# A decoder trunk on one core: three steps of the other half's background work per pair of up products instead of two, and pooling products issued one group later

## The chip, the cores and the metric

The kernel is one launch on 1 core of a Trainium2 chip. The metric is the device time of that core in microseconds (us): the median of three runs is 2252.49 us (2251.87 to 2254.62).

## What is computed

Two layers over 1040 tokens (16 learned meta tokens and 1024 inputs) with 1024 channels, all in f32. Layer 0 mixes with multi-head latent attention, layer 1 with a causal pooling mixer; each is followed by a gated MLP with a causal convolution of width 3 on the up projection. Cut to what matters here:

```python
for i in range(DEPTH):                               # DEPTH = 2
    a = rmsnorm(h, norm_mix_pre[i])
    m = mla_mixer(a, ...) if i % 2 == 0 else pool_mixer(a, w_group, scale)
    h = h + rmsnorm(m, norm_mix_post[i])
    f = conv_ffn(rmsnorm(h, norm_ffn_pre[i]), ffn_w_up[i], conv_w, conv_b, ffn_w_down[i])
    h = h + rmsnorm(f, norm_ffn_post[i])

def pool_mixer(h, w_group, scale):                   # 4 groups of 256 channels, windows 2, 4, 8, 16
    pooled[:, :, g] = mean of the last POOL_WINDOWS[g] tokens (fewer at the start)
    y = einsum('blgc,gcd->blgd', pooled - h, w_group)
    return y * scale

def conv_ffn(h, w_up, conv_w, conv_b, w_down):       # D_FF = 2816
    u = conv_b + causal width-3 convolution of (h @ w_up)
    gate, val = split(u)
    return (silu(gate) * val) @ w_down
```

## The kernel before

Channels lie on the 128 partitions, tokens on the free axis. Every f32 operand of a product is split into a high and a low part (ACT casts the high part, DVE subtracts to get the low part), and a product of two tiles is three matmuls: high by high, low weight with high data, high weight with low data. So each weight tile that arrives (`wtile`, line 702) costs one cast on ACT (`wh`) and one subtraction on DVE (`wl`), four buffers each.

From line 599 on the program treats the tokens as two halves, half 0 with 536 and half 1 with 504. For each layer and half, `ffn_up` makes the 22 channel tiles of the gated product in two parts of 11 pairs (one gate and one value tile); a pair is two up products on PE and, on DVE, two `wl`, four convolution steps `cv`, one multiplication and one `gl`. `ffn_down` follows each part. While PE works on one half, the other half's non-matrix work (normalisations, residual additions, the pooling mixer) is a generator in the list `bg`; each call of `tick` (line 639) advances it to its next `yield`, at a raised priority, and `drain` runs what is left. `ffn_up` ticks twice in a pair of products. The generator of a half at the layer boundary is `after_ffn`: `post` (line 817, 8 steps), one norm (4 steps), `poolmix` (line 973, 12 steps), then `post` and one norm again.

A norm is `inv_rms_a` (line 75: eight tiny matmuls into `ps_st`, then some ten short DVE operations) and `inv_rms_b` (line 103: two diagonal tiles `diag`, one on DVE and one on POOL, which two or four matmuls into `ps_bc` spread over the partitions; ACT copies the result to `R`). `poolmix` makes, for each of the eight channel tiles, a scaled tile `pa`, one to four running sums `psm`, the difference `pmx` and its parts `xh` and `xl`; after two tiles come the products of that group (`pool` below: matmuls whose operands are `xh`, `xl`, `pwh`, `pwl`), and ACT reads them out into `F`.

The order on each engine is fixed when the program is built: a scheduler places the instructions by priority, and on the chip each engine takes its instructions in that order. Two more sizes matter: the sums of half 1 have six banks of PSUM, those of half 0 three double ones; and the pooling weights have one buffer.

Two places at the layer boundary come up below. Stage A is `ffn_up` of half 1, part 0, layer 0, with half 0's layer boundary behind it (about 1040 to 1200 us). Stage B is `ffn_up` of half 0, part 0, layer 1, with half 1's (about 1440 to 1630 us). A third, stage 0, is `ffn_up` of half 0, part 0, layer 0 (about 620 to 760 us), which has half 1's `after_mixer` behind it.

Of the kernel before, what the change touches and what calls it, by code (L numbers as in the profile page):

```python
# [11 lines left out]
F32 = mybir.dt.float32  # L12
F32R = mybir.dt.float32r
I32 = mybir.dt.int32
ALU = mybir.AluOpType
# [6 lines left out]
KD = D // 128  # L22
# [7 lines left out]
HALF = 536  # L30
# [9 lines left out]
G_MIXPRE, G_MIXPOST, G_FFNPRE, G_FFNPOST = 0, 16, 32, 48  # L40
G_QN, G_KVN, G_PS = 64, 67, 69
G_CONV = 77
G_CNT = G_CONV + 2 * 2 * NJ * 4
# [3 lines left out]
class Kern:  # L47
# [551 lines left out]
    def dense(self):  # L599
        tc, nc, io, ctx = self.tc, self.nc, self.io, self.ctx  # L600
        P = lambda name, bufs, **kw: ctx.enter_context(tc.tile_pool(name=name, bufs=bufs, reuse_waits="tile", **kw))
        self.wp, self.ab, self.hp, self.gp = P("wp", 4), P("ab", 1), P("hp", 1), P("gp", 1)
        self.fp, self.up, self.tp = P("fp", 8), P("up", 2), P("tp", 5)
        stp = P("stf", 2, space=PSUM)
        self.stps = lambda name: stp.tile([128, 512], F32, tag="st", name=name)
        self.psum = None
        self.banks(1)
        self.dtile = lambda x: self.tp.tile([128, HALF], F32R, tag="x" + x, name="diag", bufs=2)
        self.H, self.A, self.bg = {}, {}, []

        F, acc = self.wo(0)
        self.bg.append(self.after_mixer(0, F, acc, 0, True))
        F, acc = self.wo(1)
        self.drain()
        self.bg.append(self.after_mixer(1, F, acc, 0, False))
        for L in range(2):
            self.L = L
            for hf in range(2):
                self.banks(2 - hf)
                Fa = None  # L620
                for part in range(2):
                    G = self.ffn_up(hf, part)
                    self.drain()
                    if part == 1 and hf == 0:
                        self.bg.append(self.pre(1, L))
                    if part == 1 and hf == 1 and L == 0:
                        self.bg.append(self.pre(0, 1))
                    if (L, hf, part) == (1, 1, 1):
                        self.ffn_down_last(part, G, Fa)
                        break  # L630
                    F, acc = self.ffn_down(part, G, Fa)
                    Fa = F
                    self.drain()
                else:
                    self.bg.append(self.after_ffn(hf, F, acc, L))
        self.drain()
# [13 lines left out]
    def after_mixer(self, hf, F, acc, L, pre):  # L650
        acc = yield from self.post(hf, F, acc, G_MIXPOST + 8 * L)
        if pre:

            self.late = yield from self.inv_rms_steps(acc, "xh", 2)
            yield from self.pre(hf, L, True)
        else:
            yield from self.ffn_norm(hf, acc)
# [220 lines left out]
    def ffn_up(self, hf, part):  # L878
        nc, io, L = self.nc, self.io, self.L
        ah, al = self.A[hf]  # L880
        gh, gl = [], []

        cut = hf == 0 and L == 1
        skip = DEAD - 2 if cut else 0
        pad = 2 if cut or hf else 0
        n = ah[0].shape[1] - skip - pad
        for jj in range(JH):
            j = part * JH + jj
            cv = []
            for gv in range(2):  # L890
                idx = gv * NJ + j
                u, = self.mm_half(self.wtile(io["w_up"][L, j, :, gv], KD), ah, al, skip=skip)
                if (L, hf) == (0, 0):
                    t = self.up.tile([128, HALF], F32, tag="u", name="u")
                    nc.vector.tensor_tensor(t, u, self.late, op=ALU.mult)
                    u = t
                p0 = G_CONV + (L * 2 * NJ + idx) * 4
                c = self.tp.tile([128, HALF], F32, tag="t", name="cv")[:, :n]
                nc.scalar.activation(c, u[:, pad:pad + n], AF.Identity, bias=self.par(p0 + 3), scale=self.par(p0 + 2))  # L899
                for x in (1, 0):  # L900

                    o = max(0, 2 - x - pad)
                    nc.vector.scalar_tensor_tensor(c[:, o:], u[:, pad + x - 2 + o:pad + x - 2 + n], self.par(p0 + x),  # L903
                                                   c[:, o:], op0=ALU.mult, op1=ALU.add)
                cv.append(c)
                if gv == 0:
                    nc.scalar.activation(c, c, AF.Silu)  # L907
                    self.tick()
            nc.vector.tensor_tensor(cv[0], cv[0], cv[1], op=ALU.mult)  # L909
            hi = self.gp.tile([128, HALF], F32R, tag=f"gh{jj}", name="gh")[:, :n]  # L910
            lo = self.gp.tile([128, HALF], F32R, tag=f"gl{jj}", name="gl")[:, :n]
            self.split(cv[0], hi, lo, lo_eng="dve")
            gh.append(hi)
            gl.append(lo)
            self.tick()
        return gh, gl
# [56 lines left out]
    def poolmix(self, hf, R):  # L973
        nc, io = self.nc, self.io
        F, acc = [], None
        n_tok = HALVES[hf][1]
        end = n_tok + 16
        for g in range(4):
            win = 2 << g
            xh, xl = [], []  # L980
            for kk in range(2):
                k = 2 * g + kk
                a = self.tp.tile([128, HALF + 16], F32, tag="tc", name="pa")[:, :end]
                if hf == 0:
                    nc.gpsimd.memset(a[:, :16], 0.0)
                else:
                    nc.gpsimd.tensor_scalar(a[:, :16], self.phalo[:, k], 1.0, 0.0, op0=ALU.mult, op1=ALU.add)
                nc.vector.scalar_tensor_tensor(a[:, 16:], self.H[hf][k], self.par(G_MIXPRE + 8 + k), R,
                                               op0=ALU.mult, op1=ALU.mult)
                if hf == 0:  # L990
                    nc.gpsimd.tensor_scalar(self.phalo[:, k], a[:, n_tok:end], 1.0, 0.0,
                                            op0=ALU.mult, op1=ALU.add)
                s = a
                for l in range(g + 1):
                    d = 1 << l
                    lo, hi = 2 * d - 1, end
                    n = self.tp.tile([128, HALF + 16], F32, tag="tc", name="psm")[:, :end]
                    nc.vector.tensor_tensor(n[:, lo:hi], s[:, lo:hi], s[:, lo - d:hi - d], op=ALU.add)
                    s = n
                mx = self.tp.tile([128, HALF + 16], F32, tag="tc", name="pmx")[:, :end]  # L1000
                nc.vector.scalar_tensor_tensor(mx[:, 16:], s[:, 16:], 1.0 / win, a[:, 16:],
                                               op0=ALU.mult, op1=ALU.subtract)
                if hf == 0:
                    nc.vector.tensor_tensor(mx[:, 16:32], s[:, 16:32], self.par(G_CNT + 16 * g, 16), op=ALU.mult)
                    nc.vector.tensor_tensor(mx[:, 16:32], mx[:, 16:32], a[:, 16:32], op=ALU.subtract)
                hi_ = self.tp.tile([128, HALF], F32R, tag="xh", name="xh", bufs=2)[:, :n_tok]
                lo_ = self.tp.tile([128, HALF], F32R, tag="xl", name="xl", bufs=2)[:, :n_tok]
                self.split(mx[:, 16:], hi_, lo_, lo_eng="dve")
                xh.append(hi_)
                xl.append(lo_)  # L1010
                if kk == 0:
                    W = self.wtile(io["w_pool"][g], 4, True)
                yield
            for m in range(2):
                ps = self.mm_half([W[2 * kk + m] for kk in range(2)], xh, xl)
                f = self.fp.tile([128, HALF], F32, tag="F", name="F")[:, :n_tok]
                self.evac(f, ps, self.par(G_PS + 2 * g + m))
                F.append(f)
                acc = self.addsq(acc, f)
            yield  # L1020
        return F, acc


# [50 lines left out]
```

## Time and profile before

| | |
|---|---|
| median of three runs | 2252.49 us (2251.87 to 2254.62) |
| the profiled execution | 2249.77 us, of which 2247.6 us are its span |
| PE busy | 2154.6 us, 96% of the span |
| DVE busy | 1473.8 us, 66% |
| ACT busy | 1048.6 us, 47% |
| POOL busy | 415.5 us, 18% |
| mean granted TensorE clock | 0.983 of full |

The span is the time from the first to the last instruction on the core; 2.2 us of the run's own time lie outside it. A busy engine is not the same as a needed one: the averages go over stages with different limits.

### The profile page before, as it was taken

What the parts mean: (1) busy time and instruction counts of PE and PEld (TensorE: products, weight loads), DVE (VectorE), ACT (ScalarE), POOL (GpSimd) and SP (SyncE); (2) the same over time, 40 slices, a digit from 0 to 9 for tenths busy, and PEclk for the clock granted to TensorE, in tenths of its full rate; (3) what the DMA queues carried; (4) which work ended last, traced back from release to release, by engine and by line L of the source; (5) the groups of instructions that cost most, each with busy time, mean ns of one, the idle gap of its engine ahead of it and who ended that gap; (6) DMA issues with size and microseconds to landing.
All of it is one profiled execution on the core that took longest, in us unless ns stands there. A gap on an engine that the chain in (4) does not pass through costs nothing.

```text
span 2247.6 us, 36505 instructions
## 1 busy us (share of the span) xinstructions
PE 2154.6 (96%) x13968; PEld 1968.5 (88%) x13968; DVE 1473.8 (66%) x2830; ACT 1048.6 (47%) x1934; POOL 415.5 (18%) x755
## 2 busy tenths in 40 slices
PE   8889999998999999999998999999899999999996
PEld 8778888897989999999886888899899998888886
DVE  7867777776388725765887555587745557634655
ACT  6466777776354423443544344344433433433431
POOL 6667676764000000000000000000000000000001
PEclk9989999998999999999999999999999999999998
DMA  5011111114343232233222332422242245223321
GB/s 162 15 44 26 33 30 33 30 55 125 122 159 124 77 99 98 85 95 117 91 80 92 131 101 84 132 79 86 81 135 90 72 132 178 86 84 112 98 91 46
DMA packets 82903, 202.76 MB, mean 90 GB/s; under 512 B 10548, under 2 KB 31668, under 8 KB 82728
## 3 DMA queue, kind: packets, MB, share of 16 engines
q1 hardware_dynamic: 82584, 200.18, 28.5%
q8 instruction: 110, 1.80, 0.3%
q14 instruction: 65, 0.53, 0.1%
q10 hardware_dynamic: 144, 0.25, 0.0%
HBM read 179.15 MB, written 16.97 MB: 87 GB/s over the span
## 4 chain that ended last, share of the span: by engine, by line
PE 85%; DVE 6%; ACT 3%; POOL 2%; issue 2%; DMA 2%; DVEq 0%; SPq 0%; ACTq 0%; POOLq 0%
PE ps_m L756 72%; PE ps_t L577 2%; PE ps_s L525 1%; PE ps_o L562 1%; PE ps_o L563 1%; PE ps_s L527 1%; PE ps_s L526 1%; ACT P L540 1%; PE ps_qk L408 1%; POOL P L545 1%; PE ps_qk L410 1%; DMA xt<-in_x 1%; PE ps_qk L409 1%; PE ps_st L82 1%; DVE ps_s L534 1%
## 5 line engine op out<-in xcount | busy, mean ns | idle before, releaser
L70 DVE TENSOR_TENSOR wl<-wr,wh 128x1024 fp32r<-128x1024 f32 (+3 forms) x316 | 349.3, 1105 | 419.6 <-ACT wh L64 408.6
L64 ACT CAST wh<-wr 128x1024 fp32r<-128x1024 f32 (+3 forms) x316 | 301.2, 953 | 590.8 <-PE ps_m L756 524.1
L756 PE MATMUL ps_m<-ah,wh 128*128 128x506 f32 (+2 forms) x2112 | 563.9, 321 | 3.4 <-ACT cv L899 1.7
L756 PE MATMUL ps_m<-al,wh 128*128 128x506 f32 (+2 forms) x2112 | 566.7, 322 | 0.0
L756 PE MATMUL ps_m<-ah,wl 128*128 128x506 f32 (+2 forms) x2112 | 563.1, 321 | 0.0
L756 PEld LDWEIGHTS ps_m<-ah,wh 128*128 128x128 f32 x2112 | 353.1, 189 | 35.0 <-ACT cv L899 1.9
L756 PEld LDWEIGHTS ps_m<-al,wh 128*128 128x128 f32 x2112 | 352.8, 189 | 28.2 <-issue 0.7
L756 PEld LDWEIGHTS ps_m<-ah,wl 128*128 128x128 f32 x2112 | 353.1, 189 | 27.8 <-issue 0.5
L756 PE MATMUL ps_m<-gh,wh 128*128 128x268 f32 (+3 forms) x1088 | 288.7, 318 | 1.9 <-ACT F L765 1.9
L756 PE MATMUL ps_m<-gh,wl 128*128 128x268 f32 (+3 forms) x1088 | 287.8, 317 | 0.0
L756 PE MATMUL ps_m<-gl,wh 128*128 128x268 f32 (+3 forms) x1088 | 287.3, 317 | 0.0
L903 DVE SCALAR_TENSOR_TENSOR cv<-ps_m,params,cv 128x504 f32<-128x504 f32 (+1 forms) x264 | 195.9, 744 | 3.2
L756 PEld LDWEIGHTS ps_m<-gh,wh 128*128 128x128 f32 x1088 | 182.9, 189 | 16.0 <-ACT F L765 2.1
L756 PEld LDWEIGHTS ps_m<-gh,wl 128*128 128x128 f32 x1088 | 181.9, 188 | 14.2 <-issue 0.5
L756 PEld LDWEIGHTS ps_m<-gl,wh 128*128 128x128 f32 x1088 | 182.1, 189 | 13.1
L115 POOL TENSOR_TENSOR diag<-ident,yl 65x260 fp32r<-65x260 f32 (+5 forms) x27 | 33.5, 1241 | 714.5 <-DVE yl L70 675.3
L64 ACT CAST gh<-cv 128x504 fp32r<-128x504 f32 (+2 forms) x88 | 54.6, 622 | 168.8 <-DVE cv L909 168.8
L540 ACT ACTIVATE P<-ps_s,stat 116x116 f32<-116x116 f32 (+9 forms) x160 | 111.3, 697 | 38.4 <-DVE stat L538 28.1
L577 PE MATMUL ps_t<-ident,P 116*116 116x116 f32 x720 | 118.5, 269 | 7.8 <-DVE ptl L591 4.2
L545 POOL TENSOR_SCALAR P<-P,stat 116x116 f32<-116x116 f32 (+2 forms) x144 | 108.8, 757 | 59.0 <-DVE stat L543 47.3
L907 ACT ACTIVATE cv<-cv 128x504 f32<-128x504 f32 (+2 forms) x88 | 55.8, 634 | 135.2 <-DVE cv L903 135.2
L534 DVE CUSTOM_DVE_ANT_0 ps_s<-ps_s,mask 116x116 f32<-116x116 f32 (+7 forms) x128 | 89.9, 704 | 22.6 <-PE ps_s L527 12.1
(200 smaller groups left out, 3624.3 us busy)
## 6 DMA issues: line engine op xcount, KB each, us to landing
wr<-in_w_up SPq DMA_DIRECT2D x176, 512.0 KB, 3.5
wr<-in_w_down SPq DMA_DIRECT2D x56, 384.0 KB, 3.1
wr<-in_w_down SPq DMA_DIRECT2D x56, 320.0 KB, 2.9
wr<-in_w_o SPq DMA_DIRECT2D x16, 512.0 KB, 4.0
resid<-H SPq DMA_DIRECT2D x16, 268.0 KB, 4.3
H<-resid SPq DMA_DIRECT2D x16, 268.0 KB, 3.1
xt<-in_x SPq DMA_DIRECT2D x32, 130.0 KB, 2.2
resid<-H SPq DMA_DIRECT2D x16, 252.0 KB, 3.6
```

Of the source, the lines that this page charges most:

```text
L64: nc.scalar.copy(hi, src)
L70: eng.tensor_tensor(lo, src, hi.bitcast(F32), op=ALU.subtract)
L82: nc.tensor.matmul(ps[:w, i:i + 1], acc[:, w * i:w * i + w], self.ones, start=True, stop=True)
L115: eng.tensor_tensor(t, self.ident[:w, :w].unsqueeze(1).broadcast_to([w, n, w]), part.bitcast(F32).unsqueeze(2).broadcast_to([w, n, w]), op ...
L408: nc.tensor.matmul(ps, wh, xh, start=i == 0, stop=False)
L534: nc.vector.tensor_tensor_reduce(out=ps, in0=ps, in1=self.mask[:n, o:o + nb * cn].rearrange("p (b c) -> p b c", b=nb), op0=ALU.add, op1=AL ...
L540: nc.scalar.activation(dst, ps, AF.Exp, bias=nm[:n], scale=SCALE, accum_out=es[:n, gi:gi + 1])
L545: nc.gpsimd.tensor_scalar(P[:n, :nk], P[:n, :nk], rs[:n], 1.0, op0=ALU.mult, op1=ALU.mult)
L577: nc.tensor.transpose(pt[:kn, x * QT:x * QT + n], Pi[:n, k0:k0 + kn], self.ident[:n, :n])
L756: nc.tensor.matmul(p, w, x[k][:, skip + c0:skip + c0 + m], start=k == 0 and w is wh and x is xh, stop=k == last and w is wl)
L903: nc.vector.scalar_tensor_tensor(c[:, o:], u[:, pad + x - 2 + o:pad + x - 2 + n], self.par(p0 + x), c[:, o:], op0=ALU.mult, op1=ALU.add)
L907: nc.scalar.activation(c, c, AF.Silu)
```

## The change

`ffn_up` makes each up product in two calls of four weight tiles each, and in the value product of a pair one more `tick` stands between the two, so a pair has three. The matmuls of a product and their order within it are the same. In `poolmix` the body for one channel tile becomes `shape`, and the loop runs one round more: the products of a group stand behind the first tile of the next group, which leaves nine `yield`s instead of twelve. The temporary `u` moves from a pool of its own to the tag `xl`, and `xh` and `xl` have three buffers instead of two. Lines of the changed file lie some lines lower (the convolution is line 907 instead of 903, `pa` 992 instead of 988, `psm` 1002 instead of 998).

```diff
@@ dense
-        self.fp, self.up, self.tp = P("fp", 8), P("up", 2), P("tp", 5)
+        self.fp, self.tp = P("fp", 8), P("tp", 5)
...
-        self.dtile = lambda x: self.tp.tile([128, HALF], F32R, tag="x" + x, name="diag", bufs=2)
+        self.dtile = lambda x: self.tp.tile([128, HALF], F32R, tag="x" + x, name="diag", bufs=3)
@@ ffn_up
-                u, = self.mm_half(self.wtile(io["w_up"][L, j, :, gv], KD), ah, al, skip=skip)
+                W = self.wtile(io["w_up"][L, j, :, gv], KD)
+                ps = self.mm_half(W[:KD // 2], ah, al, 0, KD, skip=skip, n=n + pad)
+                if gv == 1:
+                    self.tick()
+                u, = self.mm_half(W[KD // 2:], ah, al, KD // 2, KD, ps, skip, n + pad)
                 if (L, hf) == (0, 0):
-                    t = self.up.tile([128, HALF], F32, tag="u", name="u")
+                    t = self.tp.tile([128, HALF], F32, tag="xl", name="u", bufs=3)
@@ poolmix (shape(g, kk) holds the old body for one channel tile, unchanged but for bufs=3)
+        X = [([], []) for _ in range(4)]
+        W = None
+        for g in range(5):
             for kk in range(2):
+                if g < 4:
+                    for dst, t in zip(X[g], shape(g, kk)):
+                        dst.append(t)
+                    yield
+                if g and kk == 0:
+                    for m in range(2):
+                        ps = self.mm_half([W[2 * x + m] for x in range(2)], *X[g - 1])
+                        f = self.fp.tile([128, HALF], F32, tag="F", name="F")[:, :n_tok]
+                        self.evac(f, ps, self.par(G_PS + 2 * (g - 1) + m))
+                        F.append(f)
+                        acc = self.addsq(acc, f)
+                if g < 4 and kk == 0:
                     W = self.wtile(io["w_pool"][g], 4, True)
-                yield
...
+        yield
         return F, acc
```

What this does to the order on the engines is shown at three places, in rows that name line, operation, result, operands and size; `x2` means that two equal ones follow each other.

First, PE in stage 0, at the norm whose scale is `R` for half 1's up operand. Before, its sums stand inside an up product:

```order
L756 MATMUL ps_m_10378<-al_9384,wh_10373 128x268 x2
L82 MATMUL ps_st_10200<-ones_66,acc_9841 63x1 x8
L756 MATMUL ps_m_10378<-ah_9383,wl_10374 128x268 x2
L756 MATMUL ps_m_10378<-ah_9389,wh_10373 128x268 x2
L756 MATMUL ps_m_10378<-al_9390,wh_10373 128x268 x2
```

and the norm's first `ps_bc` matmul follows 146 up matmuls later. In the changed program, at the end of a product, stands:

```order
L756 MATMUL ps_m_10247<-al_9447,wh_10242 128x268 x2
L756 MATMUL ps_m_10247<-ah_9446,wl_10243 128x268 x2
L82 MATMUL ps_st_10003<-ones_66,acc_9741 63x1 x8
L122 MATMUL ps_bc_10109<-diag_10105,ones_r_68 128x504
L122 MATMUL ps_bc_10109<-diag_10107,ones_r_68 128x504
L756 MATMUL ps_m_10309<-ah_9368,wh_10304 128x268 x2
```

The 146 up matmuls between the two halves of the norm are gone from there; they stand behind it.

Second, PE in stage A, at the norm before `poolmix`. Before, the spreading matmuls are followed by the rest of their up product and by two more products, 54 matmuls, ahead of the first pooling matmul, and 53 up matmuls stand between the sums and the spreading:

```order
L756 MATMUL ps_m_14420<-al_13362,wh_14415 128x506
L122 MATMUL ps_bc_14406<-diag_14402,ones_r_68 128x268
L122 MATMUL ps_bc_14410<-diag_14402,ones_r_68 128x268
L756 MATMUL ps_m_14420<-ah_13361,wl_14416 128x506
L122 MATMUL ps_bc_14406<-diag_14404,ones_r_68 128x268
L122 MATMUL ps_bc_14410<-diag_14404,ones_r_68 128x268
L756 MATMUL ps_m_14420<-ah_13453,wh_14415 128x506
```

In the changed program 14 up matmuls stand between the sums and the spreading, and the first pooling matmuls follow at once:

```order
L756 MATMUL ps_m_14391<-ah_13459,wl_14387 128x506
L122 MATMUL ps_bc_14251<-diag_14247,ones_r_68 128x268
L122 MATMUL ps_bc_14255<-diag_14247,ones_r_68 128x268
L122 MATMUL ps_bc_14251<-diag_14249,ones_r_68 128x268
L122 MATMUL ps_bc_14255<-diag_14249,ones_r_68 128x268
L756 MATMUL ps_m_14421<-xh_14305,pwh_14329 128x268
L756 MATMUL ps_m_14422<-xh_14305,pwh_14329 128x268
L756 MATMUL ps_m_14440<-xh_14305,pwh_14329 128x268
L756 MATMUL ps_m_14441<-xh_14305,pwh_14329 128x268
L756 MATMUL ps_m_14488<-ah_13190,wh_14483 128x506
```

From there to the last pooling matmul of the half PE had 240 other matmuls (222 of up products and 18 of the down product) among the 96 of pooling; now it has 98.

Third, DVE in stage A, in the third pooling group. Before, the tiles of `poolmix` alternate with the convolution and the weight splits of the up products:

```order
L988 SCALAR_TENSOR_TENSOR pa_14893<-H_13853,params_70,R_14401 128x536
L903 SCALAR_TENSOR_TENSOR cv_14884<-ps_m_14859,params_70,cv_14884 128x504
L1004 TENSOR_TENSOR pmx_14839<-psm_14837,params_70 128x16
L998 TENSOR_TENSOR psm_14897<-pa_14893 128x551
L909 TENSOR_TENSOR cv_14824<-cv_14824,cv_14884 128x504
L1005 TENSOR_TENSOR pmx_14839<-pmx_14839,pa_14829 128x16
L70 TENSOR_TENSOR wl_15300<-wr_15298,wh_15299 128x640
L998 TENSOR_TENSOR psm_14899<-psm_14897 128x549
```

In the changed program they follow each other there:

```order
L1002 TENSOR_TENSOR psm_14594<-psm_14592 128x545
L1005 SCALAR_TENSOR_TENSOR pmx_14596<-psm_14594,pa_14586 128x536
L992 SCALAR_TENSOR_TENSOR pa_14640<-H_13852,params_70,R_14246 128x536
L1008 TENSOR_TENSOR pmx_14596<-psm_14594,params_70 128x16
L1002 TENSOR_TENSOR psm_14644<-pa_14640 128x551
L1009 TENSOR_TENSOR pmx_14596<-pmx_14596,pa_14586 128x16
L1002 TENSOR_TENSOR psm_14646<-psm_14644 128x549
L70 TENSOR_TENSOR xl_14601<-pmx_14596,xh_14600 128x536
L1002 TENSOR_TENSOR psm_14648<-psm_14646 128x545
```

From the first `pa` to the last `xl` of the half DVE had 107 rows (81 wide ones of 500 to 551 columns, 16 of 16 columns, 6 `wl` of 1024 and 4 of 768 or 640 columns); now it has 82 (62 wide, 16 small, 4 `wl` of 1024). In stage B the same stretch has 77 rows instead of 103 on DVE (71 wide and 6 `wl` now), and 301 up matmuls instead of 658 others among the 48 of pooling on PE.

## Rows read from the trace of the kernel before

**Rows 1.** The page: the span, and the engines' busy time.

```profile
span 2247.6 us, 36505 instructions
PE 2154.6 (96%) x13968; PEld 1968.5 (88%) x13968; DVE 1473.8 (66%) x2830; ACT 1048.6 (47%) x1934; POOL 415.5 (18%) x755
```

**Rows 2.** Waits of PE from 1170 to 1260: total, times, longest.

```profile
PE ps_m L756 <- DVE psm L998: 10.1, 1, 10.1
PE ps_m L756 <- ACT xh L64: 2.3, 1, 2.3
```

**Rows 3.** Waits of PE from 1450 to 1660, same columns.

```profile
PE ps_m L756 <- ACT xh L64: 2.7, 1, 2.7
PE ps_m L756 <- ACT F L765: 1.9, 1, 1.9
PE ps_m L756 <- DVE xl L70: 1.2, 1, 1.2
```

**Rows 4.** Timeline of PE, 1160 to 1230: start, us, what.

```profile
1174.49 0.62 PE L756 MATMUL ps_m<-al,wh 128*128 128x506 f32 x1
1174.91 0.63 PE L756 MATMUL ps_m<-ah,wl 128*128 128x506 f32 x1
...
1193.40 1.26 PE L756 MATMUL ps_m<-xh,pwh 128*128 128x268 f32 x4 [10.13 <-DVE psm L998]
...
1196.95 0.40 PE L756 MATMUL ps_m<-gh,wh 128*128 128x504 f32 x1
```

**Rows 5.** Stretches by engine: busy (instructions), granted clock, DMA share, GB/s.

```profile
1119.30:1198.10 78.80, 66.36 (x311) 55.89 (x309) 66.89 (x109) 37.09 (x62) 3.53 (x15) 0.91 0.23 68
1300.00:1350.00 50.00, 50.00 (x220) 41.25 (x219) 29.59 (x36) 21.43 (x28) 0.00 (x0) 1.00 0.29 95
```

**Rows 6.** Timeline, 605 to 620: a norm with DVE otherwise idle.

```profile
608.43 1.08 PE L82 MATMUL ps_st<-ones,acc 128*67 128x1 f32 x16
609.54 0.16 DVE L84 TENSOR_SCALAR nv<-ps_st 67x8 f32<-67x8 f32 x1 [0.88 <-PE ps_st L82]
...
612.23 1.42 POOL L115 TENSOR_TENSOR diag<-ident,yl 67x536 fp32r<-67x536 f32 x1 [65.98 <-DVE yl L70]
...
617.72 0.41 PE L122 MATMUL ps_bc<-diag,ones_r 67*128 67x268 f32 x2
...
619.23 1.47 DVE L824 SCALAR_TENSOR_TENSOR F<-F,params,R 128x536 f32<-128x536 f32 x2 [4.06 <-ACT R L124]
```

**Rows 7.** Timeline, 594 to 597: a weight split behind a product's end.

```profile
594.90 1.05 ACT L64 CAST wh<-wr 128x1024 fp32r<-128x1024 f32 x1 [3.58 <-PE ps_m L756]
...
595.98 1.23 DVE L70 TENSOR_TENSOR wl<-wr,wh 128x1024 fp32r<-128x1024 f32 x1 [3.91 <-ACT wh L64]
```

**Rows 8.** Timeline of PE at the program's last norm.

```profile
2236.49 0.94 PE L122 MATMUL ps_bc<-diag,ones_r 31*128 31x248 f32 x2 [6.94 <-DVE diag L115]
```

**Rows 9.** Timeline of DVE and ACT in the pooling mixer of stage A.

```profile
1119.94 0.78 DVE L988 SCALAR_TENSOR_TENSOR pa<-H,params,R 128x536 f32<-128x536 f32 x1 [0.96 <-ACT R L124]
...
1121.88 1.21 DVE L70 TENSOR_TENSOR wl<-wr,wh 128x1024 fp32r<-128x1024 f32 x1
1123.02 0.71 DVE L1001 SCALAR_TENSOR_TENSOR pmx<-psm,pa 128x536 f32<-128x536 f32 x1
...
1183.67 0.68 DVE L909 TENSOR_TENSOR cv<-cv 128x504 f32<-128x504 f32 x1
...
1192.71 0.64 ACT L64 CAST xh<-pmx 128x536 fp32r<-128x536 f32 x1 [6.30 <-DVE pmx L1005]
1193.38 0.72 DVE L70 TENSOR_TENSOR xl<-pmx,xh 128x536 fp32r<-128x536 f32 x1
...
1197.37 0.72 DVE L70 TENSOR_TENSOR xl<-pmx,xh 128x536 fp32r<-128x536 f32 x1 [0.71 <-ACT xh L64]
```

**Rows 10.** Timeline of PE in stage B; 12 matmuls start between the two rows' starts.

```profile
1510.91 0.41 PE L756 MATMUL ps_m<-ah,wh 128*128 128x260 f32 x2
...
1512.38 0.41 PE L756 MATMUL ps_m<-ah,wh 128*128 128x260 f32 x2
```

More of the change, by code (lines that the diff above doesn't have):

```diff
@@ L652, in after_mixer @@
         if pre:
-            self.late = yield from self.inv_rms_steps(acc, "xh", 2)
+            self.late = yield from self.inv_rms_steps(acc, "xh", 3)
             yield from self.pre(hf, L, True)
@@ L977, in poolmix, with shape @@
         end = n_tok + 16
-        for g in range(4):
+        def shape(g, kk):
             win = 2 << g
-            xh, xl = [], []
-            for kk in range(2):
[L982 to L1011, printed above, removed]
-                    W = self.wtile(io["w_pool"][g], 4, True)
-                yield
[L1014 to L1020, printed above, removed]
@@ new lines, in shape @@
+            k = 2 * g + kk
+            a = self.tp.tile([128, HALF + 16], F32, tag="tc", name="pa")[:, :end]
+            if hf == 0:
+                nc.gpsimd.memset(a[:, :16], 0.0)
+            else:
+                nc.gpsimd.tensor_scalar(a[:, :16], self.phalo[:, k], 1.0, 0.0, op0=ALU.mult, op1=ALU.add)
+            nc.vector.scalar_tensor_tensor(a[:, 16:], self.H[hf][k], self.par(G_MIXPRE + 8 + k), R,
+                                           op0=ALU.mult, op1=ALU.mult)
+            if hf == 0:
+                nc.gpsimd.tensor_scalar(self.phalo[:, k], a[:, n_tok:end], 1.0, 0.0,
+                                        op0=ALU.mult, op1=ALU.add)
@@ new lines, in shape @@
+            s = a
+            for l in range(g + 1):
+                d = 1 << l
+                lo, hi = 2 * d - 1, end
+                n = self.tp.tile([128, HALF + 16], F32, tag="tc", name="psm")[:, :end]
+                nc.vector.tensor_tensor(n[:, lo:hi], s[:, lo:hi], s[:, lo - d:hi - d], op=ALU.add)
+                s = n
+            mx = self.tp.tile([128, HALF + 16], F32, tag="tc", name="pmx")[:, :end]
+            nc.vector.scalar_tensor_tensor(mx[:, 16:], s[:, 16:], 1.0 / win, a[:, 16:],
+                                           op0=ALU.mult, op1=ALU.subtract)
@@ new lines, in shape @@
+            if hf == 0:
+                nc.vector.tensor_tensor(mx[:, 16:32], s[:, 16:32], self.par(G_CNT + 16 * g, 16), op=ALU.mult)
+                nc.vector.tensor_tensor(mx[:, 16:32], mx[:, 16:32], a[:, 16:32], op=ALU.subtract)
+            hi_ = self.tp.tile([128, HALF], F32R, tag="xh", name="xh", bufs=3)[:, :n_tok]
+            lo_ = self.tp.tile([128, HALF], F32R, tag="xl", name="xl", bufs=3)[:, :n_tok]
+            self.split(mx[:, 16:], hi_, lo_, lo_eng="dve")
+            return hi_, lo_
```

## The prediction

> **What bounds the kernel now.** The page comes first: PE is busy for 2154.6 of 2247.6 us and no other engine comes near it [rows 1], so the kernel is bound by PE and a change can win only where PE stands still or runs at the lower clock. Then the waits of PE, stage by stage. In stage A there are two, 2.3 and 10.1 us, both for pooling operands [rows 2]; in stage B I count 2.7, 1.9 and 1.2 us [rows 3]; in stage 0 none that counts. Third, the timeline of PE around such a wait. In front of the 10.13 us wait stands a pooling matmul, and the down products behind it stay behind it; after it the matmuls run at half pace until 1196.95 [rows 4]. The pace is read from starts: 0.42 us from one 506-column matmul to the next at 1174.49 against 50 / 220 = 0.227 us in an undisturbed stretch whose granted clock is 1.00 [rows 4, 5]; the levels are 1.2 and 2.4 GHz. From 1193.40 to 1196.95 are 3.55 us at half pace, so 1.7 us of work are lost behind such a wait.
>
> So stage A loses 2.3 + 10.1 + 2 x 1.7 = 15.8 us, and stage B 2.7 + 1.9 + 1.2 + 1.7 = 7.5 us (one fall of the clock). These 23.3 us are all that the change can win.
>
> The Trainium skill, page "PSUM — Partial Sum Buffer", section "Engine vs sequencer instructions", says that the queues of ACT, DVE and POOL are strictly first in, first out, and that matmuls start and complete in program order. The trace agrees: for 10.13 us PE passed nothing by [rows 4]. By that rule the place of a matmul in the order counts, and it speaks against this change, which puts waiting matmuls closer behind what they wait for.
>
> **What DVE can do.** The pooling mixer is work for DVE. The stretch in stage A from the first `pa` (1119.94) to the last `xl` (1198.09) has 107 rows [rows 9], 66.9 us of them busy in 78.8 us [rows 5]. A step is taken from starts, since neighbours overlap a little: from 1183.67 to 1193.38 DVE starts 14 wide rows and 2 small ones in 9.71 us [rows 9]; with 0.15 for a small one a wide one takes 0.672 us. A `wl` of 1024 columns takes 1.14 us (1121.88 to 1123.02) [rows 9]. The sum for the 107 rows, 81 x 0.672 + 16 x 0.15 + 6 x 1.14 + 4 x 0.85 (the narrower `wl`, by width) = 67.1 us, meets the 66.9 us busy.
>
> **The change, part by part.**
>
> Splitting an up product into two calls, the new tags and the third buffers add no instruction on any engine: nothing to pay. What counts is that 50% more ticks pull the other half's work forward by priority, and where that puts it.
>
> *Stage 0.* The sums of the norm now stand at a product's end, and the two spreading matmuls directly behind them, in place of 146 up matmuls between (some 18 us). Nothing is left to cover the chain. Bare, it takes from 609.54 (`nv`) to 613.65 (POOL's `diag` done), 4.1 us [rows 6]. Ahead of `nv` DVE's queue now holds a `wl` whose buffer and cast wait for the end of that same product: cast and subtraction end 597.21 - 594.90 = 2.3 us after it [rows 7]. The sums themselves take 0.95 us of PE. So PE waits 2.4 + 4.1 + 0.1 - 0.95 = 5.6 us, and loses 1.7 us of pace behind it: **+7.3 us**. Behind the spreading matmul stands the whole rest of the up products, and no other work is ready for PE. The lower bound is the bare chain, 4.1 + 1.7 = 5.8; the upper the same adjacency at the program's end, where PE waited 6.94 us [rows 8], + 1.7 = 8.6.
>
> *Stage A.* Count from the end of the sums of the norm ahead of `poolmix`.
> - The spreading: covered by 14 up matmuls, 14 x 0.227 = 3.2 us. DVE needs the bare chain, 4.1, and between its rows one `wl`, one `gl` and two `cv`, 1.14 + 3 x 0.672 = 3.2: ready at 7.3, so PE waits 4.1 us.
> - The first pooling matmul follows the spreading with no cover. `R` is usable 619.23 - 617.72 = 1.5 us after the spreading's start [rows 6], at 8.8. Up to the first `xh` stand five wide and two small rows on DVE and the cast of 0.64 us on ACT [rows 9]: 3.4 + 0.3 + 0.7 = 4.4. PE is through with the spreading at 8.1 and starts at 13.2: 5.1 us of waiting.
> - From `R` to the last `xl` DVE now has 82 rows: 62 x 0.672 + 16 x 0.15 + 4 x 1.14 = 48.7 us, so the last `xl` comes at 57.5 at the earliest. DVE has waits of its own in such a stretch (for casts on ACT, for sums that PE has not ended, for the one pooling weight buffer): before, 78.2 - 66.9 = 11 us over 107 rows, which by rows is 8 for 82. The last pooling matmuls can start at 65.5; without any waits at 57.5, with all 11 at 68.5.
> - PE's own work up to there: 112 up matmuls x 0.227 = 25.5, 84 pooling matmuls of 268 columns x 0.12 (an estimate by width from 0.227 for 506) = 10.1, the spreading 0.8: 36.4 us. PE loses 65.5 - 36.4 = 29 us, the two waits above among them (bounds 21 and 32, with 3.4 for the clock at the upper one, 35).
>
> Before, PE had 240 other matmuls in this stretch, 54 us, to cover 67 us of DVE; now it has 98, 22 us, to cover 49. The rows that left the stretch on DVE are 25, the matmuls that left it are 142. The pooling work is done earlier, and the 15.8 us of waiting at the end of the stage go with it, but DVE's queue is the limit in the middle. What comes behind (`post` and the second norm inside `ffn_up`) is covered: 46 rows, some 32 us, beside 10 us left of two products, three products of 5.5 and the first down products. The sum is 29 - 15.8 = **+13 us**, bounds +5 and +19.
>
> *Stage B.* The norm keeps 75 matmuls of 0.1225 us [rows 10], 9.2 us, of cover, for the chain of 4.1 and a `wl`, a `gl` and two `cv`, some 7.3 us: no loss. From `R` (1 us behind the spreading) DVE has 71 wide rows of 504 columns (0.63 us each, an estimate by width) and 6 `wl`: 51.5 us, with 4 us of waits (half as much as in A, since an up product here lasts 48 x 0.1225 = 5.9 us and the half has no small rows). PE has 301 x 0.1225 + 44 x 0.227 = 46.9 us. PE loses 56.5 - 46.9 = 9.6, and some of the pace, against 7.5 before: **+3 us**, bounds -3 (no waits on DVE: 5.6, no fall of the clock) and +8.
>
> The sum is 7.3 + 13 + 3 = +23 us on the profiled execution's own 2249.77 us, 2273. The median of the runs shown is 2.7 us above that execution, so I forecast 2276 us.
>
> **The rivals.**
> - *The drain goes and nothing takes its place* (the other side). The waits of stages A and B are where the mixer arrives too late; moved forward by 50% more ticks it is ready in time: 2252.5 - 23.3 = 2229 us. It decides if DVE can do its 82 rows in PE's 36 us, at most 0.44 us a row; the rows give 0.59. For it speaks that DVE is 66% busy on the whole [rows 1]. The Trainium skill, page "Perfetto Trace Analysis", section "Optimization Strategy", says that interleaving regimes with different limits can improve performance; that is this case, and [rows 5] show 12 us of DVE idle in the stretch that it could use. Chance 6%.
> - *The waits only change places.* In A and B the loss stays what it was, since DVE's whole work is the same, and only stage 0 is new: 2252.5 + 7.3 = 2260 us. It needs DVE to run without waits of its own in A (+5) and B to gain 3. Chance 14%.
> - *It is worse.* The late `wl` and the PSUM banks that pooling sums hold also stop the up products between the pooling groups, and PE runs most of the 65 us of stage A at half pace: all upper bounds, 8.6 + 19 + 8 = 36, and some more: 2292 us. Chance 12%.
> - That the change does not do what it says is excluded by the order.
>
> **How the numbers follow.** The forecast, +23, has 68%. The range goes by the bounds: low 5.8 + 5 - 3 = +8, 2261; high +36, 2289. Within 0.2% (4.5 us, about what a measurement of this kernel can tell from no change) and faster get little: faster 6%, same 4% (the lower end of the second rival), slower 90%.
>
> **What the changed profile would show.** In stage 0 a wait of PE of 5 to 6 us at `ps_bc` for a `diag`, in a place that had none. In stage A waits at `ps_bc` (about 4), at the first pooling matmul for `xh` (about 5), and several in the third and fourth pooling groups for `xl` and `xh`, 25 to 30 us together, with DVE more than 85% busy; and none at the down product. In stage B some 8 to 10 us in the pooling groups. I am wrong if DVE's rows in stage A end within some 45 us of `R`, if PE shows no wait between the sums and the spreading in stage 0, or if the waits at the start of the down products remain as well.

## The result and the profile after

The changed kernel takes 2277.14 us in the median of four runs (2274.51 to 2277.97), beside 2252.43 us (2251.87 to 2254.62) for the kernel before on the same chip: a ratio of 1.0104, interval 1.0090 to 1.0117. It is slower by 24.7 us; 2276 was forecast.

The page's first lines, which answer to [rows 1]:

```profile
span 2275.4 us, 36478 instructions
PE 2168.9 (95%) x13968; PEld 1980.0 (87%) x13968; DVE 1471.2 (65%) x2830; ACT 1049.5 (46%) x1934; POOL 419.9 (18%) x755
```

Nothing was added: the engines have almost the instructions and the busy time that they had, but for 14 us more on PE, which its lower pace makes of the same matmuls. So the 27.8 us between the two spans are waits and pace of PE. To see where, I use four marks that all but one of these programs have on their chain of waits: the first sums of a norm (`ps_st`, start and us) of half 1 in stage 0, and the first in half 1 of layer 0, in half 0 of layer 1 and in half 1 of layer 1. Between two of them PE has nearly the same work in every kernel. The kernel before:

```profile
666.54 1.01 PE ps_st L82 x16
...
1052.39 0.92 PE ps_st L82 x16
...
1447.84 1.01 PE ps_st L82 x16
...
1866.13 0.89 PE ps_st L82 x16
```

The changed kernel:

```profile
670.55 1.01 PE ps_st L82 x16
...
1062.43 0.92 PE ps_st L82 x16
...
1472.38 1.01 PE ps_st L82 x16
...
1893.89 0.89 PE ps_st L82 x16
```

The stretch with stage 0 takes 391.88 us in place of 385.85 (+6.0), the one with stage A 409.95 in place of 395.45 (+14.5), the one with stage B 421.51 in place of 418.29 (+3.2); from the last mark to the end both take 381.5 us. That is +23.7. The other 4.0 us lie ahead of the first mark, where the change moves nothing: there the profiled executions of eleven other kernels lie between 667.54 and 670.82, and the one before happens to be the earliest. The medians agree with 24.7.

The waits of PE in the changed kernel (total, times, longest), in stage 0, in stage A and in stage B:

```profile
PE ps_bc L122 <- DVE diag L115: 4.0, 1, 4.0
...
PE ps_m L756 <- ACT xh L64: 15.7, 4, 5.4
PE ps_bc L122 <- DVE diag L115: 3.2, 1, 3.2
PE ps_m L756 <- DVE xl L70: 1.8, 1, 1.8
PE ps_bc L122 <- POOL diag L115: 0.4, 1, 0.4
...
PE ps_m L756 <- ACT xh L64: 5.0, 2, 3.1
PE ps_m L756 <- DVE cv L907: 1.6, 2, 1.1
PE ps_m L756 <- DVE xl L70: 1.2, 2, 0.7
PE ps_m L756 <- ACT F L767: 1.0, 2, 0.7
```

In stage A the 10.1 us in front of the down products [rows 2, 4] are gone, and 21.1 us stand in place of 12.4. The timeline of PE shows in which order (start, us, what, in brackets the idle time ahead of it and its releaser); the last row is the first of the last tile's pooling matmuls:

```profile
721.59 1.08 PE L82 MATMUL ps_st<-ones,acc 128*63 128x1 f32 x16
...
726.72 1.68 PE L122 MATMUL ps_bc<-diag,ones_r 63*128 63x504 f32 x2 [4.05 <-DVE diag L115]
...
1114.88 1.08 PE L82 MATMUL ps_st<-ones,acc 128*67 128x1 f32 x16
...
1122.45 0.51 PE L122 MATMUL ps_bc<-diag,ones_r 67*128 67x268 f32 x2 [3.17 <-DVE diag L115]
1123.39 0.51 PE L122 MATMUL ps_bc<-diag,ones_r 67*128 67x268 f32 x2 [0.43 <-POOL diag L115]
...
1129.28 1.26 PE L756 MATMUL ps_m<-xh,pwh 128*128 128x268 f32 x4 [5.38 <-ACT xh L64]
...
1158.97 1.26 PE L756 MATMUL ps_m<-xh,pwh 128*128 128x268 f32 x4 [4.67 <-ACT xh L64]
...
1162.04 0.81 PE L756 MATMUL ps_m<-xl,pwh 128*128 128x268 f32 x2 [1.81 <-DVE xl L70]
...
1167.64 1.26 PE L756 MATMUL ps_m<-xh,pwh 128*128 128x268 f32 x4 [3.44 <-ACT xh L64]
...
1172.86 1.26 PE L756 MATMUL ps_m<-xh,pwh 128*128 128x268 f32 x4 [2.17 <-ACT xh L64]
...
1183.07 0.54 PE L756 MATMUL ps_m<-xh,pwh 128*128 128x268 f32 x3
```

In stage 0 the chain of waits shows what the spreading is now waiting through, piece by piece (small DVE steps left out):

```profile
718.00 3.35 PE ps_m L756 x27
...
721.38 1.05 ACT wh L64
...
722.46 1.23 DVE wl L70
723.68 0.08 DVE nv L84
...
726.24 1.32 POOL diag L115
...
727.61 0.79 PE ps_bc L122
```

A weight's cast on ACT, which waits for the end of the product that just ran, and its subtraction on DVE stand ahead of `nv`, and 3.9 us from `nv` to the end of POOL's `diag` follow: the chain that the prediction put together from [rows 6, 7].

### The profile page after: what moved, and what is told of

Read it like the earlier page. It is cut to its first block, busy times and chain, and to the rows that moved or that the text cites. A ratio compares the mean times of both kernels' runs of the same rounds, so it can differ in the third digit from the quotient of the medians.

```text
span 2275.4 us, 36478 instructions
## 1 busy us (share of the span) xinstructions
PE 2168.9 (95%) x13968; PEld 1980.0 (87%) x13968; DVE 1471.2 (65%) x2830; ACT 1049.5 (46%) x1934; POOL 419.9 (18%) x755
## 4 chain that ended last, share of the span: by engine, by line
PE 85%; DVE 6%; ACT 3%; issue 2%; DMA 2%; POOL 2%; DVEq 0%; ACTq 0%; SPq 0%; POOLq 0%
PE ps_m L756 71%; PE ps_t L577 2%; PE ps_s L525 1%; PE ps_o L562 1%; PE ps_o L563 1%; PE ps_s L527 1%; PE ps_s L526 1%; ACT P L540 1%; PE ps_qk L408 1%; PE ps_qk L409 1%; PE ps_qk L410 1%; DMA xt<-in_x 1%; DVE ps_s L534 1%; PE ps_bc L122 1%; PE ps_st L82 1%
## 5 line engine op out<-in xcount | busy, mean ns | idle before, releaser
L70 DVE TENSOR_TENSOR wl<-wr,wh 128x1024 fp32r<-128x1024 f32 (+3 forms) x316 | 348.4, 1102 | 452.1 <-ACT wh L64 448.8
L64 ACT CAST wh<-wr 128x1024 fp32r<-128x1024 f32 (+3 forms) x316 | 301.1, 953 | 585.4 <-PE ps_m L756 501.9
L64 ACT CAST gh<-cv 128x504 fp32r<-128x504 f32 (+2 forms) x88 | 54.7, 623 | 169.5 <-DVE cv L913 169.4
L903 ACT ACTIVATE cv<-ps_m,params 128x504 f32<-128x504 f32 (+1 forms) x132 | 101.7, 770 | 18.4 <-PE ps_m L756 18.4
```

What stands on the lines that cost most here:

```text
L64: nc.scalar.copy(hi, src)
L70: eng.tensor_tensor(lo, src, hi.bitcast(F32), op=ALU.subtract)
```

## The experiments

The change is taken apart first (the first four kernels), then its parts are varied. The rival to the prediction's account of stage A is that only latency counts: each pooling product stands right behind the chain that makes its operands, and DVE's total work has little to do with it.

### The new pooling order alone

Two ticks a pair in their old places, a whole up product; the pooling loop and the three buffers as in the change.

```diff
-                W = self.wtile(io["w_up"][L, j, :, gv], KD)
-                ps = self.mm_half(W[:KD // 2], ah, al, 0, KD, skip=skip, n=n + pad)
-                if gv == 1:
-                    self.tick()
-                u, = self.mm_half(W[KD // 2:], ah, al, KD // 2, KD, ps, skip, n + pad)
+                u, = self.mm_half(self.wtile(io["w_up"][L, j, :, gv], KD), ah, al, skip=skip)
```

> The changed kernel without the third tick and without the split of the up product: of the change only the pooling order (and the buffers it needs) is left. My theory, that the pace of the ticks does the harm: stage A keeps 231 up matmuls beside its pooling matmuls and 105 rows on DVE, as before, so 2252 us, or up to 6 us less, since three steps fewer are left to drain. The rival, that products issued behind the next group's first tile wait longer in themselves: some 2262 to 2267 us, with most of the +14.5 us of stage A.

Measured: 2247.61 us (2245.88 to 2248.66), 0.9975 of before (0.9964 to 0.9986). By the marks nothing in stage 0, -6.6 us in A, +1.6 in B. This half of the change pays; the price is the other half's.

### The third tick alone

The changed `ffn_up`, with the pooling loop of before (products right behind their group's second tile).

```diff
-                if g < 4:
-                    for dst, t in zip(X[g], shape(g, kk)):
-                        dst.append(t)
-                    yield
...
+            for m in range(2):
+                ps = self.mm_half([W[2 * kk + m] for kk in range(2)], xh, xl)
```

> The changed kernel with the old pooling order: the third tick (inside a split product) and the buffers are left. My theory: stage 0 loses its 6 us just the same (sums and spreading adjacent). In stage A DVE has 92 rows beside 163 up matmuls, a better balance than 82 beside 98, but the norm's spreading stands directly behind its sums, so the loss there stays, +8 to +14 us; stage B gains up to 4 or stays. Together 2260 to 2270 us. The rival, that the pooling order is what costs: about 2258 us, the 6 us of stage 0 alone.

Measured: 2293.77 us (2290.53 to 2295.35), 1.0176 (1.0161 to 1.0191), 24 us above the upper end of what I expected; +6.9 in stage 0, +25.8 in A, +7.4 in B. PE's timeline in stage A, same columns as above:

```profile
1118.06 1.75 PE L122 MATMUL ps_bc<-diag,ones_r 67*128 67x268 f32 x4 [6.53 <-DVE diag L115]
...
1125.09 1.26 PE L756 MATMUL ps_m<-xh,pwh 128*128 128x268 f32 x4 [5.28 <-ACT xh L64]
...
1146.49 1.26 PE L756 MATMUL ps_m<-xh,pwh 128*128 128x268 f32 x4 [4.97 <-ACT xh L64]
...
1169.92 1.26 PE L756 MATMUL ps_m<-xh,pwh 128*128 128x268 f32 x4 [7.36 <-ACT xh L64]
...
1193.71 1.26 PE L756 MATMUL ps_m<-xh,pwh 128*128 128x268 f32 x4 [7.52 <-ACT xh L64]
```

Each of the four groups now waits for its own `xh`. So the new pooling order is worth 5 us at two ticks (2252.7 to 2247.6), but 16.6 beside the third (2293.8 to 2277.1). The parts don't add up: they share the waits.

### Neither: the split product and the buffers alone

```diff
-                if gv == 1:
-                    self.tick()
                 u, = self.mm_half(W[KD // 2:], ah, al, KD // 2, KD, ps, skip, n + pad)
```

(and the pooling loop of before, and the tick behind `silu` kept)

> Neither the third tick nor the new pooling order: the product in two calls, u under the tag of xl, three buffers. My theory: nothing, 2252 us within 2. The rival, that the split or the shared buffers (u beside the low diagonal) cost something by themselves: 2255 to 2260 us, with waits of PE for DVE's u in stage 0.

Measured: 2252.06 us (2250.33 to 2253.70), 0.9995 (0.9986 to 1.0005). Costing these edits at nothing was right.

### The change without the third tick in stage 0

```diff
-                if gv == 1:
+                if gv == 1 and (L, hf) != (0, 0):
                     self.tick()
```

> The whole change, but two ticks per pair in layer 0, half 0. My theory: only stage 0 comes back, 75 up matmuls stand between sums and spreading there: 6 us less than the changed kernel, 2271 us, with stages A and B as they are in it. The rival, that the 6 us of stage 0 are work that moved and returns elsewhere: 2277 us.

Measured: 2268.71 us (2266.33 to 2270.47), 1.0063 (1.0047 to 1.0080): 8.4 us below the change in the medians. By the marks stage 0 is back to nothing, A has +14.1 and B +3.4 as in the change. So stage 0 costs 6 us by the marks and 8 by the medians; the forecast of 7.3 lies between them.

### The change with the pooling's `xl` on POOL

This takes 8 subtractions of a half, some 0.7 us each, from DVE.

```diff
-            self.split(mx[:, 16:], hi_, lo_, lo_eng="dve")
+            self.split(mx[:, 16:], hi_, lo_, lo_eng="pool")
```

> The whole change, but the eight low parts xl of each half's pooling mixer are subtracted on POOL instead of DVE. My theory, that DVE's queue sets the length of stage A: eight wide rows less, 8 x 0.672 = 5.4 us, in A, and up to as much in B: 2268 to 2273 us. The rival, that PE waits for the latency of the chain from R to each pair of operands and not for DVE's throughput: POOL takes about 1.4 us for a row that takes DVE 0.7, so nothing is won or some us are lost, 2277 to 2282 us.

Measured: 2280.37 us (2279.12 to 2281.53), 1.0118 (1.0103 to 1.0133): not faster than the change, 3 us above it in the medians (the intervals overlap). Two windows from `R` to just ahead of the last `xl` (length, then busy time and instructions of PE, weight loads, DVE, ACT, POOL, and PE's granted clock); first the changed kernel, then this one:

```profile
1124.50:1179.00 54.50, 37.63 (x161) 32.09 (x162) 47.58 (x81) 22.13 (x39) 9.36 (x15) 0.72 0.20 68
```

```profile
1124.50:1182.00 57.50, 40.64 (x174) 34.26 (x175) 47.75 (x74) 22.54 (x39) 16.20 (x22) 0.73 0.19 64
```

The second stretch is 3 us longer. But rows left DVE and time did not: it is busy for 47.75 us with 74 rows, in place of 47.58 with 81. Rows of DVE that run beside a subtraction on POOL got longer. One of POOL's subtractions and the DVE row beside it:

```profile
1128.99 1.78 POOL L70 TENSOR_TENSOR xl<-pmx,xh 128x536 fp32r<-128x536 f32 x1 [0.52 <-ACT xh L64]
```

```profile
1129.50 1.30 DVE L1008 TENSOR_TENSOR pmx<-psm,params 128x16 f32<-128x16 f32 x1
```

The same row in the changed kernel:

```profile
1130.45 0.17 DVE L1008 TENSOR_TENSOR pmx<-psm,params 128x16 f32<-128x16 f32 x1
```

Five places on DVE in this window are 0.7 to 1.1 us longer in this way, 4.9 us together, and the seven subtractions that left it took 5.0. So the time is the one that I gave the rival, but the run does not decide between the two: it took no time from DVE, and a subtraction that takes 1.3 to 2.8 us on POOL also makes the chain longer than DVE's 0.72.

### Two ticks, one of them inside the value product

The change without the tick behind `silu`.

```diff
                 if gv == 0:
                     nc.scalar.activation(c, c, AF.Silu)
-                    self.tick()
```

> The whole change, but two ticks per pair: the one behind the gate product's silu is left out, the one inside the value product stays. My theory, that the number of ticks does the harm: as with two ticks in the old places and the new pooling order, 2248 us within 3. The rival, that a tick in the middle of a product is what hurts (its work goes ahead of the product's second half): over 2260 us.

Measured: 2240.63 us (2238.84 to 2241.18), 0.9940 (0.9925 to 0.9955). The number of ticks makes the loss, as expected; but the place counts too, which I had not expected: 7 us below the new order with the ticks in their old places.

### The third tick in every second pair

```diff
-                if gv == 1:
+                if gv == 1 and jj % 2 == 0:
                     self.tick()
```

> The whole change, but the third tick in every second pair only. My theory: between the two in stage A, 88 rows of DVE (some 54 us, with its waits 62) beside 127 up matmuls and the pooling, 41 us: a loss of 20 us there, 4 to 8 more than before; stage 0 still has sums and spreading adjacent, +6; stage B is about even or 4 better: 2258 to 2266 us. The rival, that the harm comes from the uncovered first norm of the mixer alone, which has 53 matmuls of cover here: 2253 us or less.

Measured: 2270.73 us (2268.80 to 2272.05), 1.0074 (1.0059 to 1.0089), 5 us above my range. This kernel's chain of waits lacks the marks; by the starts of the same sums in PE's timeline, in both kernels: +5.8 in stage 0, +7.8 in A, +3.3 in B. Half the additional ticks cost all of stage 0 and B and half of A: what decides in stage 0 is that the spreading again stands directly behind the sums, and PE waits 4.18 us there.

### The new order at two ticks, with `xl` on POOL

The first experiment's kernel with the edit of the fifth.

> The new pooling order with two ticks per pair in their old places, and xl on POOL. My theory: stage A still loses some 9 us of PE there to DVE; a part of eight wide rows, 2 to 4 us, comes back: 2244 to 2246 us. The rival, that POOL's longer latency is met by PE at each group: 2248 to 2253 us.

Measured: 2243.46 us (2242.12 to 2244.69), 0.9952 (0.9935 to 0.9969), 4 us better than without the edit; by the marks 2.1 of them in A and 1.5 in B. Over the whole program DVE is busy for 1467.1 us in place of 1472.0: 16 subtractions of 0.7 us, some 11 us, left it, and its time fell by 4.9. How much of the 4 us comes from DVE's shorter time and how much from the other order of the rows is not shown.

### One tick inside, and `xl` on POOL

The sixth experiment's kernel with the edit of the fifth.

> Two ticks a pair, the second one inside the value product, new pooling order, and the low parts of the pooling operands on POOL in place of DVE. Theory (at two ticks DVE's rows still cost something): the same gain as beside the new order alone, 4 us, from 2240.6 to 2236.5 us. Rival (with the tick inside the product only 2.8 and 0.9 us of PE's waiting are left in stage A, so nothing is to be had): 2239 to 2242 us, and the waits for xh become waits for POOL's xl.

Measured: 2233.12 us (2232.27 to 2234.07), 0.9908 (0.9893 to 0.9923): better than both kernels, and better than I expected. The window of [rows 5] again:

```profile
1119.30:1198.10 78.80, 78.80 (x388) 66.86 (x387) 70.68 (x108) 40.62 (x67) 20.66 (x23) 1.00 0.25 77
```

PE is busy through all of the 78.8 us at full clock, with DVE at 70.7, and the view of its waits in stage A is empty. By the marks A gains 16.0 us and B 3.6. The prediction put the loss of the kernel before in A at 15.8.

The 7.5 us that this kernel is below the sixth are for the most part not a saving of DVE's time: over the whole program it is busy for 1469.2 us in place of 1472.3. The stretch from the first `pa` to the last `xl` in stage A, in the sixth kernel and in this one:

```profile
1120.45:1195.10 74.65, 70.89 (x341) 59.86 (x340) 67.08 (x112) 37.14 (x61) 5.95 (x15) 0.98 0.26 78
```

```profile
1122.50:1194.25 71.75, 71.75 (x353) 60.89 (x353) 66.72 (x104) 37.14 (x61) 20.66 (x23) 1.00 0.27 84
```

With eight rows fewer DVE is busy only 0.4 us less; the stretch is 2.9 us shorter because DVE stands still for 5.0 us in place of 7.6. The 3.7 us of waits that PE had left in stage A (2.8 and 0.9) are gone. What DVE no longer waits for is the cast of a pooling weight on ACT: in the sixth kernel that stretch has `DVE pwl L70 <- ACT pwh L64: 5.4, 2, 2.9` (total, times, longest), in this one no such wait. Why that cast now comes in time stays open.

### The tick inside, with the old pooling order

The kernel before with the split product and its tick moved from behind `silu` to the middle of the value product.

> The kernel before with the tick behind the silu moved into the value product, in the middle of it: two ticks a pair, the old pooling order. Theory (the place of the tick pays by itself, 7 us as between the two kernels with the new pooling order): 2245 to 2247 us, with the wait of 10 us at the first down product shorter. Rival (the place pays only where the products of a group stand one tile later): 2251 to 2254 us.

Measured: 2257.50 us (2255.76 to 2260.52), 1.0018 (1.0009 to 1.0027): the rival's side, and a little worse than it said. By the marks 2.7 us are won in A and 9.8 lost in B. The mixer's end is late in both, in A as in the kernel before (first row), and now in B too (second row):

```profile
1194.83 1.26 PE L756 MATMUL ps_m<-xh,pwh 128*128 128x268 f32 x4 [9.79 <-ACT xh L64]
...
1602.36 1.21 PE L756 MATMUL ps_m<-xh,pwh 128*128 128x504 f32 x2 [7.83 <-DVE pa L991]
```

So the place pays only beside the new pooling order. Why the mixer ends later in B here than in the kernel before stays open.

### The change with the first pooling products later

Three ticks, with six empty steps ahead of the first group's products, so that 54 up matmuls cover the first pooling matmul and 53 the spreading.

```diff
                     yield
+                    if (g, kk) == (1, 0):
+                        yield
+                        yield
+                        yield
+                        yield
+                        yield
+                        yield
```

> The changed kernel, three ticks a pair, with six empty steps ahead of the first pooling group's products: in stage A 53 up matmuls again cover the norm's spreading and 54 the first pooling matmul, 161 up matmuls stand in the stretch instead of 98, and DVE has 93 rows in it. By the sum of the prediction (sums, chain, 93 rows of 0.6 us, 8 us of DVE's own waits against 72 us of PE's work) PE loses 17 us in stage A instead of 29: 2277 - 12 = 2265 us. Rival (three ticks a pair cost what they cost wherever the first products stand, and the waits only move to the later groups): 2275 to 2279 us.

Measured: 2263.89 us (2261.69 to 2266.12), 1.0046 (1.0034 to 1.0059): the prediction's 2265. By the marks +7.0 in stage 0, +5.0 in A, +1.0 in B. All waits of PE in stage A:

```profile
1170.80 1.26 PE L756 MATMUL ps_m<-xh,pwh 128*128 128x268 f32 x4 [5.52 <-ACT xh L64]
...
1173.28 0.82 PE L756 MATMUL ps_m<-xl,pwh 128*128 128x268 f32 x2 [1.21 <-DVE xl L70]
...
1179.73 1.26 PE L756 MATMUL ps_m<-xh,pwh 128*128 128x268 f32 x4 [4.30 <-ACT xh L64]
...
1184.95 1.26 PE L756 MATMUL ps_m<-xh,pwh 128*128 128x268 f32 x4 [2.16 <-ACT xh L64]
```

The first three waits of the changed kernel (3.17 + 0.43 + 5.38 = 9.0 us) are gone and the four behind them are nearly as they were, 13.2 us in place of 12.1. Stage A got 9.5 us shorter. So the waits did not move: those at the start of the stage are a cost of their own, one that cover takes away. The wait at the spreading follows the cover: 6.53 us with no up matmul between sums and spreading (the second experiment), 3.17 us with 14, which are 3.2 us of work, and none with 53.

## Why the prediction was right

The time was right (2276 against 2277.1), and its three terms came out near what they forecast, the third in part by luck:

- **Stage 0**, +7.3 (5.8 to 8.6): +6.0 by the marks, and the experiment without it gives 6 to 8 back. The wait is 4.05 us, not 5.6: I let both spreading matmuls wait for POOL's `diag`, but the first one needs DVE's alone and runs while POOL's is made. The second still starts no earlier than the chain allows (727.61, 6.3 us after the product's end at 721.35; I had 2.4 + 4.1 = 6.5). The Trainium skill, page "PSUM — Partial Sum Buffer", section "Engine vs sequencer instructions", says that matmuls start and complete in program order, and the trace agrees: in these 4.05 us no up matmul went past the waiting spreading.
- **Stage A**, +13 (5 to 19): +14.5. The places of the waits are those of the prediction: 3.2 + 0.4 at the spreading (4.1 said), 5.4 at the first pooling matmul (5.1), the rest in the last groups, none at the down product. The last tile's pooling matmuls start at 1183.07, 67.1 us after the sums end at 1115.96 (65.5). With 36.4 us of PE's own work at full pace that is a loss of 30.7 us (29): 21.1 us of waits and, by difference, 9.6 us of pace, at a granted clock of 0.72 in the window from 1124.50 to 1179.00. So the 25 to 30 us of waits that I said the profile would show were too many, and the slower pace is the rest. Less the 15.8 us of before, 30.7 is +14.9.
- **Stage B**, +3 (-3 to +8): +3.2, with 8.8 us of waits of PE. The view of [rows 3] has two more rows, which I left out, one of 0.3 us and this one:

```profile
PE ps_m L756 <- ACT cv L899: 1.7, 1, 1.7
```

The kernel before thus had 7.8 us of waits in stage B, not 5.8, and they rose by 1.0 only. The other 2.1 us are pace: between the marks PE is busy for 412.73 us in place of 410.59 over the same 3283 matmuls. My sum had the waits before 2.0 us too low and left most of the pace unpriced.

The rivals fell: the drain did go, but its cost came back earlier in the same stage (2229 us was the time if it had not), A's loss did not stay what it was (2260), and the time is 15 us below that of the third rival (2292).

**How far its account of stage A is shown.** "DVE's queue is the limit in the middle" agrees with the trace of the changed kernel. The window over the later part of the stretch, and the two rows of DVE that bound it:

```profile
1139.97:1178.69 38.72, 26.63 (x114) 22.52 (x113) 37.72 (x62) 17.88 (x31) 8.07 (x9) 0.74 0.29 95
```

```profile
1139.97 0.69 DVE L70 TENSOR_TENSOR pwl<-wr,pwh 128x512 fp32r<-128x512 f32 x1 [4.61 <-ACT pwh L64]
...
1179.39 0.72 DVE L70 TENSOR_TENSOR xl<-pmx,xh 128x536 fp32r<-128x536 f32 x1 [0.71 <-ACT xh L64]
```

The first `pa` starts at 1124.52, 8.6 us after the sums (8.8 said), and the last `xl` ends at 1180.11, 55.6 us later: 48.3 us of 82 rows (47.58 up to 1179.00, and the last `xl` with 0.72; 48.7 said) and 7.3 us of DVE's own waits (8 said). That the waits came out is luck in part, since I carried them over from the kernel before in proportion to the rows, and 4.6 of the 7.3 are one wait for the cast of a pooling weight. From 1139.97 on DVE is busy for 37.72 of 38.72 us, and rows of the up products stand there between those of the pooling: the last four waits of PE are for a queue that hardly stands still, those at the start of the stage for chains without cover. That fewer rows on DVE would shorten the later part is argued from this and not shown: the run that took rows away, the fifth, left DVE's time as it was, and the eighth and ninth took 4.9 and 3.1 us from it over the whole program.

**What I did not see** is that the change held two opposite parts. The later pooling products alone make the kernel faster, and the third tick alone costs 41 us; I forecast their sum without parting them. The rule of the Trainium skill that I weighed as a rival (page "Perfetto Trace Analysis", section "Optimization Strategy", on interleaving work with different limits) isn't refuted: the ninth kernel, which interleaves without a wait in stage A, gains 0.9%. The change interleaved less: its pooling ran beside 98 matmuls of other work in place of 240.

## What to carry to other kernels

Background work that is advanced by raised priority can come too soon as well as too late: each step that comes earlier takes a stretch of foreground matmuls from between a chain and its consumer, and here nothing on the tensor engine went past a waiting matmul. So count, for each product of the background, the foreground matmuls between its operands' making and itself, and compare their time with the chain's: none means a wait as long as the chain, and a slower pace behind it. Put the products one step later before the steps are made to come sooner. And when rows are moved from the busy vector engine to another, compare its busy time before and after: here most of that time came back on the rows that ran beside the moved ones.

## What the runs showed that I had not expected

- The same move of eight subtractions a half from DVE to POOL gains nothing at three ticks a pair (2277.1 to 2280.4), 4 us at two (2247.6 to 2243.5) and 7.5 with one of the two inside a product (2240.6 to 2233.1). DVE's busy time in the whole program changes by +1.8, -4.9 and -3.1 us, though some 11 us of rows leave it.
- A subtraction of 128 x 536 took 1.32 to 1.37 us on POOL in three cases of the fifth experiment's stage A and 1.78 to 2.78 in five, beside 0.72 us on DVE [rows 9]; a DVE row of 16 columns beside one of them took 1.30 us in place of 0.17.
- At the same number of ticks, the place of one within a pair gains 7 us with the new pooling order and loses 4 with the old.
- Half of the additional ticks cost two thirds of the whole: 17 us of 24.7, each against the kernel before as it was measured beside it.
